# A tick of filler matmuls between the two pmx passes of quarter 2, and quarters 5, 8, 17 and 27 set to three ticks

## The chip, the cores and the metric

The kernel runs on one core of a Trainium2 chip. The metric is the device time of one execution in microseconds; shown is the median of several runs. Five engines work side by side, each through its own list of instructions in order: TensorE (PE), VectorE (DVE), ScalarE (ACT), GpSimd (POOL) and SyncE (SP), which issues most of the DMAs. An engine waits only where an instruction names a semaphore of another engine or of a DMA.

## The reference: what is computed

One layer over 1024 latent tokens (a grid of 16 rows by 64 columns) and 256 context tokens, model width 1024, all in float32. A modulated RMS norm is followed by one input projection, whose columns go to two branches: attention with 8 heads of 64 in a clamped 8x16 window, with a learned bias per offset and all context keys in the same softmax, and a gated short convolution. Each branch is multiplied by SiLU of its own gate; one output projection and a gated residual end the layer.

```python
h = rmsnorm(x, norm_g) * (1 + scale[:, None]) + shift[:, None]
q, k, v, za, u, bg, cg, zc = jnp.split(h @ w_in, SPLIT_POINTS, axis=-1)
attn = neighbourhood_attention(q, k, heads(v), kc, vc, rpb) * jax.nn.silu(za)
conv = bg * centred_short_conv(cg * u, conv_w, conv_b) * jax.nn.silu(zc)
x_new = x + gate[:, None] * (jnp.concatenate([attn, conv], axis=-1) @ w_out)
```

## The kernel before, in words

Every float32 product is made of three passes over operands split in a high and a low part (`mm3`, line 72). The program has four stages: modulation and norm of x (to about 78 us), the projections for q, k and v (to about 270 us), attention (to about 530 us), and the output projection.

**The attention stage** is a loop over n = 0 to 35 that calls `quarter(n)` (line 1074). A head has four quarters, so n = 4h + g works on quarter g of head h; and three steps of a software pipeline stand in one call. Quarter n computes new scores (PE tiles `pss` and `pc`, lines 1100 and 1105), adds the bias and keeps a running maximum (DVE, `sb` and `mx`, lines 1133 to 1141); for e = n - 2 it turns the maxima with the PE into tile `pmx` (first pass, line 1086), reduces them on DVE to `rm` (line 1088), spreads `rm` back over the partitions with the PE (second pass, line 1096), copies the result on ACT to `mg`, and takes exponentials (DVE subtractions `sc` and `sb`, ACT, low parts on POOL `plc` and DVE `pll`); for o = n - 3 it multiplies with the values (PE tile `po`). In this stage PE, ACT, DVE and POOL run in exactly the order in which the code records the instructions (`ordered`, line 44); SP's order is made by the framework's scheduler.

**The filler.** The PE work of attention is too short for the other engines' chain, so the rest of the projections (the gates z and the convolution's u, c, gate and b columns) is cut into ticks and put between. A unit (line 341) is one block of 128 columns: 8 ticks, each of two steps k with three matmuls of 512 columns, so six matmuls. Ticks 1 to 4 of a unit fill one tile `pu` (its first half of the tokens, k from 0 to 7), ticks 5 to 8 the next one. `pu` has two buffers (line 358), so tick 1 of a unit writes over the first half of the unit before. The units run in the order z0 to z3, and then for each of three convolution groups CU, CCG, ZC, CBG. `next(fill)` gives out one tick. Quarter n has `TICKS[n]` of them (line 33): from n = 1 on, one stands after the score matmuls (line 1116), the others after the `po` matmuls at the end of the quarter (line 1144). In total 110 ticks are given out.

**The chores.** A tick leaves work for other engines, put in two lists (`soon` and `slow`, line 302): ACT splits the next unit's weights (`uh<-uraw`), DVE takes the low part (`ul`), ACT copies products away (`z`, `ub`), DVE multiplies (`cu`, `cv`), ACT and DVE make the convolution's taps (`cv<-cu`), ACT applies SiLU (`zs<-pu`), for which it loads another function table and then loads the table of the exponential again. ACT does all of its chores at the end of a quarter (`do_acts`, line 1148), behind its exponentials. DVE does them early in the next quarter (`do_dves(3)`, line 1091): all of `soon` and up to three of `slow`, between `rm` and the subtraction `sc<-sc,mg`; a step of `gated` (line 1280) may add `ri`, or `zs` and `tb`, at the same place. So a tick that moves into another quarter takes its chores along.

With the table of before, 48 ticks have been given out at the end of quarter 16 and 80 at the end of quarter 26: there the first and the second ZC unit end, and the CBG units begin with quarters 17 and 27.

Of the kernel before, what the change touches and what calls it, by code (L numbers as in the profile page):

```python
# [29 lines left out]
CTXT = 3  # L30
FORDER = [4, 5, 6, 0, 1, 2, 3, 7]

TICKS = [2, 3, 3, 3, 3, 2, 3, 3, 2] + 2 * (8 * [3] + 2 * [4]) + 3 * [3] + [4, 4, 3, 2]
EPS = 1e-6


# [3 lines left out]
def body(tc, es, x, ctxt, w_ada, b_ada, w_in, q_g, k_g, rpbr, w_out, vecs, cst, out):  # L40
# [269 lines left out]
    def do_acts():  # L310
        for c in soon + (slow if not any(c[1] and c[1].__name__ == "product" for c in soon) else []):
            if c[0]:
                c[0]()
                c[0] = None

    def do_dves(most=99):
        for queue in chores:
            while queue and not queue[0][0] and (queue is soon or most > 0 and not soon):
                on_dve = queue.pop(0)[1]
                if on_dve:  # L320
                    on_dve()
                    most -= 1
# [730 lines left out]
    def pair_of(n):  # L1053

        h, g = divmod(n, 4)
        two = [(h, 0), (h - 1, 7)] if g == 0 else [(h, 2 * g - 1), (h, 2 * g)]
        return [(i, heads[h_], j) for i, (h_, j) in enumerate(two) if 0 <= h_ < NH]

    def both(v, n, pair):

        w = 256 if n % 4 == 0 else 384
        return v[:, pair[0][0]:pair[-1][0] + 1, :w]

    def maxima_of(n, pair):

        step, w = (768, 256) if n % 4 == 0 else (P, 384)
        lo = (2 * (n % 4) - 2) * P if n % 4 else pair[0][0] * step
        v = mg[:, lo:lo + w].rearrange("p (o c) -> p o c", o=1)
        if len(pair) == 1:
            return v  # L1070
        part = list(v.ap)
        return bass.AP(v.tensor, v.offset, [part[0], [step, 2], [1, w]])

    def quarter(n):

        live = lambda m: 0 <= m < 4 * NH
        ticks = TICKS[n]  # L1080
        e, o = n - 2, n - 3
        if live(e):
            hd, g = heads[e // 4], e % 4
            pm = psm.tile([P, 512], F32, name="pmx", tag="C", bufs=2)
            for i in range(2):
                pe.transpose(pm[:, i * P:(i + 1) * P], mx[:, (2 * g + i) * P:(2 * g + i + 1) * P], ident)
            rm = ap.tile([P, 2], F32, name="rm", tag="rm", bufs=8)
            dve.tensor_reduce(rm, pm[:, :256].rearrange("p (i k) -> p i k", i=2), AX.X, ALU.max)
        if live(o):
            heads[o // 4].ctx_out(o % 4)  # L1090
        do_dves(3)
        if gating and next(gating[0], "end"):
            gating.pop(0)
        if live(e):
            for i in range(2):
                pe.transpose(pm[:, 256 + i * P:256 + (i + 1) * P], rm[:, i:i + 1].broadcast_to([P, P]), ident)
            act.copy(mg[:, g * 256:(g + 1) * 256], pm[:, 256:512])
        now = pair_of(n)
        for i, hd_, j in now:
            hd_.scores(j, sbank[:, i])  # L1100
        if n == 0:
            next(fill)
            ticks -= 1
        if live(n):
            heads[n // 4].ctx_scores(n % 4)
        if live(e):
            hd.ctx_exp(g)
        if e in sbs or e in exps:
            pair, sb = pair_of(e), sbs.pop(e)
            w = both(sb, e, pair)  # L1110
            dve.tensor_tensor(w, w, maxima_of(e, pair), ALU.subtract)
            exps[e] = [ap.tile([P, 2, 384], F32R, name=m, tag=m, bufs=2) for m in ("phl", "pll")]
            ph, pl = (both(v, e, pair) for v in exps[e])
            act.activation(ph, w, AF.Exp)
            act.activation(w, w, AF.Exp)
        for _ in range(n > 0):
            next(fill, None)
        done = []
        if o >= 0:
            pho, plo = exps.pop(o)  # L1120
            for i, hd_, j in pair_of(o):
                hd_.lat_out(j, pho[:, i], plo[:, i])
                if j in (4, 7):
                    done.append((hd_, j // 7))
                    if j == 7 and hd_.s:
                        ready.append(hd_.p)
        if now:
            sb = sbs[n] = sb_new()
            g_ = n % 4
            if g_:  # L1130
                bt = now[0][1].bt
                bias = bt[:, 1:2].broadcast_to([P, 2, 384]) if g_ == 2 else bt[:, 0:2] if g_ == 1 else bt[:, 1:3]
                dve.tensor_tensor(sb, sbank[:, :, :384], bias, ALU.add)
            else:
                for i, hd_, j in now:
                    cols = slice(P, 384) if j == 0 else slice(0, 256)
                    dve.tensor_tensor(sb[:, i, :256], sbank[:, i, :256], hd_.bt[:, 1, cols], ALU.add)
            if live(n):
                heads[n // 4].ctx_max(n % 4)
            for i, hd_, j in now:  # L1140
                hd_.lat_max(j, sb[:, i])
        if e in sbs or e in exps:
            dve.tensor_tensor(pl, w, ph.bitcast(F32), ALU.subtract)
        for _ in range(ticks - (n > 0)):
            next(fill, None)
        for hd_, bank_ in done:
            hd_.finish(bank_)
        do_acts()
# [5 lines left out]
    def fillers():  # L1154
        for unit_ in [attn_group(f) for f in range(NPAIR)] + [conv_group(i) for i in range(1, 4)]:
            for got in unit_:
                if got is None:
                    yield
# [5 lines left out]
    fill = fillers()  # L1164
# [143 lines left out]
    with sbuf("att") as ap, psum("psb") as psb:  # L1308
# [6 lines left out]
        for n in range(4 * NH + 4):  # L1315
            h, g = divmod(n, 4)
            if 0 < h < NH and g == 0:
                heads[h].load_v()
            if h + 1 < NH and g:
                nx = heads[h + 1]  # L1320
                for load in ((nx.masks, nx.load_q), (nx.load_k,), ())[g - 1]:
                    load()
            quarter(n)
            if ready:
                p = ready.pop()
                if p < NPAIR - 1:
                    gating.append(gated(p))
                else:
                    recip(p, ap)
# [139 lines left out]
```

## Time and profile before

| | |
|---|---|
| median of 3 runs | 637.93 us (636.94 to 639.37) |
| the profiled execution's own time | 636.79 us |
| its span, first to last instruction | 635.0 us |
| mean granted TensorE clock | 0.999 |
| attention stage | about 270 to 530 us |

A row of the timeline gives the start in microseconds from the beginning of the span, the duration, the engine, the source line, the operation, the tiles it writes and reads with their shapes, how many equal ones were put together, and in brackets how long the engine stood idle before it and which engine's instruction ended that. Nearly all lines read L55, since the recording helper there issues every instruction: the tiles tell what it is. Matmuls overlap in the pipe, so the distance from start to start is the cost of one, not the shown duration. A quarter is recognised by its `pmx` rows: first pass `pmx<-ci,mx`, second pass `pmx<-ci,rm`; the first `pmx` rows of the stage belong to quarter 2.

### The profile page before, as it was taken

The numbers are of one execution on the slowest core, as the hardware profiler recorded it, in microseconds if no ns is written. First come the engines' busy times: TensorE is split into PE (matmuls) and PEld (weight loads), VectorE is DVE, ScalarE is ACT, GpSimd is POOL, SyncE is SP. The second block draws the span as 40 slices with busy tenths as digits, with TensorE's granted clock in tenths as the row PEclk, the third lists the DMA queues.
The fourth block names the chain that finished last, engine by engine and source line by source line (L and its number), as shares of the span: only waits on it lengthen the run. The fifth ranks groups of instructions, "written<-read, shape, count | busy, mean of one in ns | idle before, by whom it ended". The sixth has DMA issues, their size and how long they took to land.

```text
span 635.0 us, 10038 instructions
## 1 busy us (share of the span) xinstructions
PE 626.1 (99%) x3479; PEld 537.1 (85%) x3480; DVE 436.5 (69%) x819; ACT 324.1 (51%) x699; POOL 130.4 (21%) x140
## 2 busy tenths in 40 slices
PE   8999999999999999999999999999999999999997
PEld 3477899999899999888888888888888788888885
DVE  1677858765766845468898889988998964575111
ACT  3676835424624545345576658567775854451000
POOL 1305014123123222101122111111111112005221
PEclk9999999999999999999999999999999999999999
DMA  8972638866784994875383635683742233966421
GB/s 320 386 260 96 186 107 258 262 198 216 245 262 138 305 334 152 304 244 168 127 260 116 240 109 204 193 276 101 252 145 74 61 106 120 328 208 233 165 101 50
DMA packets 102863, 125.61 MB, mean 198 GB/s; under 512 B 9649, under 2 KB 71305, under 8 KB 101532
## 3 DMA queue, kind: packets, MB, share of 16 engines
q1 hardware_dynamic: 96348, 113.38, 53.9%
q10 hardware_dynamic: 6208, 11.05, 5.6%
q0 software_dynamic: 256, 0.54, 0.3%
q8 instruction: 27, 0.44, 0.3%
q14 instruction: 24, 0.20, 0.1%
HBM read 88.09 MB, written 38.62 MB: 200 GB/s over the span
## 4 chain that ended last, share of the span: by engine, by line
PE 91%; DVE 6%; ACT 1%; issue 1%; POOL 0%; DVEq 0%; ACTq 0%; POOLq 0%
PE pu L55 25%; PE pacc L55 21%; PE po L55 7%; PE acc L55 7%; PE tr L55 5%; PE pout L75 5%; PE pout L74 5%; PE pout L76 5%; PE cacc L55 4%; PE pss L55 3%; PE pmx L55 2%; DVE mx L55 2%; PE pc L55 2%; DVE sb L55 2%; PE trA L55 1%
## 5 line engine op out<-in xcount | busy, mean ns | idle before, releaser
L55 PE MATMUL pu<-h,uh 128*128 128x512 f32 x544 | 169.0, 392 | 0.0
L55 PE MATMUL pacc<-wh,h 128*128 128x384 f32 x512 | 135.1, 338 | 0.0
L55 PEld LDWEIGHTS pu<-h,uh 128*128 128x128 f32 x544 | 98.1, 188 | 16.9
L55 PE MATMUL pu<-h,ul 128*128 128x512 f32 x272 | 106.3, 391 | 0.0
L55 PEld LDWEIGHTS pacc<-wh,h 128*128 128x128 f32 x512 | 92.8, 188 | 0.1
L55 POOL TENSOR_TENSOR plc<-sc,phc 128x512 fp32r<-128x512 f32 x32 | 43.0, 1345 | 215.5 <-ACT sc L55 159.0
L55 PE MATMUL pacc<-wl,h 128*128 128x384 f32 x256 | 85.6, 334 | 0.0
L55 POOL TENSOR_TENSOR ss<-ss,few 128x4 f32<-128x4 f32 (+1 forms) x40 | 41.4, 1037 | 126.3 <-DVE ss L55 126.1
L55 DVE TENSOR_TENSOR mx<-mx,sb 128x384 f32<-128x384 f32 (+1 forms) x64 | 59.4, 936 | 2.0
L55 PEld LDWEIGHTS pu<-h,ul 128*128 128x128 f32 x272 | 51.1, 188 | 11.3
L75 PE MATMUL pout<-wol,yh 128*128 128x512 f32 x128 | 49.8, 389 | 0.0
L76 PE MATMUL pout<-woh,yl 128*128 128x512 f32 x128 | 49.5, 389 | 0.0
L74 PE MATMUL pout<-woh,yh 128*128 128x512 f32 x128 | 48.3, 389 | 0.0
L55 PEld LDWEIGHTS pacc<-wl,h 128*128 128x128 f32 x256 | 48.1, 188 | 0.1
L55 DVE TENSOR_REDUCE ss<-sq 128x4 f32<-128x260 f32 (+1 forms) x40 | 15.8, 394 | 42.4 <-ACT sq L55 42.4
L55 ACT ACTIVATE sq<-pacc 128x256 f32<-128x256 f32 x32 | 12.3, 384 | 54.4 <-PE pacc L55 53.9
L1401 DVE TENSOR_TENSOR ot<-pout,gate 128x512 f32<-128x512 f32 x16 | 10.8, 689 | 40.5 <-PE pout L76 37.7
L55 ACT COPY mg<-pmx 128x256 f32<-128x256 f32 x32 | 11.9, 372 | 51.9 <-PE pmx L55 45.3
L1402 POOL TENSOR_TENSOR ot<-ot,xr 128x512 f32<-128x512 f32 x15 | 20.0, 1345 | 68.2 <-DVE ot L1401 67.0
L55 ACT COPY sc<-pc 128x512 f32<-128x512 f32 x32 | 18.8, 588 | 25.5 <-PE pc L55 25.5
L55 ACT ACTIVATE qn<-pacc,ss 128x64 f32<-128x64 f32 x128 | 30.0, 329 | 3.0 <-issue 2.5
L55 DVE TENSOR_TENSOR pll<-sb,phl 128x768 fp32r<-128x768 f32 (+2 forms) x33 | 28.4, 861 | 4.5 <-ACT sb L55 4.5
(155 smaller groups left out, 1280.9 us busy)
## 6 DMA issues: line engine op xcount, KB each, us to landing
uraw<-in_w_in SPq DMA_DIRECT2D x34, 256.0 KB
q_d<-qs SPq DMA_DIRECT2D x32, 256.0 KB
k_s<-k_d SPq DMA_DIRECT2D x8, 1024.0 KB
q_s<-q_d SPq DMA_DIRECT2D x16, 512.0 KB
wr<-in_w_in SPq DMA_DIRECT2D x40, 192.0 KB
slab<-in_w_ada SPq DMA_DIRECT2D x6, 1024.0 KB
v_d<-vs SPq DMA_DIRECT2D x20, 260.0 KB
v<-v_d SPq DMA_DIRECT2D x16, 325.0 KB
```

The costliest lines, as they stand in the source:

```text
L55: i = emit(*a, **kw)
L74: i = pe.matmul(ps, ah, bh, start=first, stop=False)
L75: pe.matmul(ps, ah, bl, start=False, stop=False)
L76: pe.matmul(ps, al, bh, start=False, stop=last)
L1401: dve.tensor_tensor(ot, ps, gate[:, cols], ALU.mult)
L1402: (dve if (nh, t) == (1, NB - 1) else pool).tensor_tensor(ot, ot, xr, ALU.add)
```

## The change

The table of ticks is rewritten, and one branch is added in `quarter`:

```diff
-TICKS = [2, 3, 3, 3, 3, 2, 3, 3, 2] + 2 * (8 * [3] + 2 * [4]) + 3 * [3] + [4, 4, 3, 2]
+TICKS = [2] + 17 * [3] + [4] + 9 * [3] + [4] + 3 * [3] + [4, 4, 3, 2]
...
         if live(o):
             heads[o // 4].ctx_out(o % 4)
+        elif live(e):
+            next(fill)
+            ticks -= 1
         do_dves(3)
```

Written out, four entries differ: quarters 5 and 8 go from 2 to 3 ticks, quarters 17 and 27 from 4 to 3. The sum stays 110. So the filler is one tick ahead of before at the end of quarters 5 to 7, two at the end of 8 to 16, one at the end of 17 to 26, and level from the end of quarter 27 on. The new branch holds only for n = 2, where e = 0 exists and o = -1 does not: its first tick then stands between the two `pmx` passes, and its last one is left out.

PE in quarter 2 (`h_219` to `h_745` are the eight k of the normalised x, two to a tick):

```order
 L55 MATMUL pmx<-ci,mx 128x128 x2
+L55 MATMUL pu<-h_221,uh 128x512 x2
+L55 MATMUL pu<-h_221,ul 128x512
+L55 MATMUL pu<-h_222,uh 128x512 x2
+L55 MATMUL pu<-h_222,ul 128x512
 L55 MATMUL pmx<-ci,rm 128x128 x2
 L55 MATMUL pss<-q_s,k_s 128x384 x4
 L55 MATMUL pc<-q_s,kc_s 128x256 x4
-L55 MATMUL pu<-h_221,uh 128x512 x2
-L55 MATMUL pu<-h_221,ul 128x512
-L55 MATMUL pu<-h_222,uh 128x512 x2
-L55 MATMUL pu<-h_222,ul 128x512
```

The tick that stood behind the scores now stands before the second pass; the later ticks of the quarter follow one place earlier.

PE before, where the first CBG unit begins (`h_219` is k = 0): its first tick comes in quarter 17, behind the scores, and its first matmul waits for ACT.

```order
L55 MATMUL pss<-q_s,k_s 128x384 x4
L55 MATMUL pc<-q_s,kc_s 128x256 [waits PE_49]
L55 MATMUL pc<-q_s,kc_s 128x256 x3
L55 MATMUL pu<-h_219,uh 128x512 [waits Activation_49]
L55 MATMUL pu<-h_219,uh 128x512
L55 MATMUL pu<-h_219,ul 128x512
```

PE in the change: the same tick comes in quarter 16, behind that quarter's `po` matmuls (`h_745` is k = 7, the last step of the ZC unit).

```order
L55 MATMUL pu<-h_745,ul 128x512
L55 MATMUL po<-phl,v_3356 65x384 [waits Activation_49]
L55 MATMUL po<-phl,v_3356 65x384
L55 MATMUL po<-pll,v_3356 65x384
L55 MATMUL po<-phl,v_3356 65x384 x2
L55 MATMUL po<-pll,v_3356 65x384
L55 MATMUL pu<-h_219,uh 128x512 [waits Activation_49]
```

ACT in the change, quarter 16 from the copy of the context scores on, to the first row of quarter 17:

```order
L55 COPY sc<-pc 128x512 [waits PE_49,Pool_49]
L55 ACTIVATE phc<-sc 128x512 [waits DVE_49]
L55 ACTIVATE sc<-sc 128x512 [waits Activation_49]
L55 ACTIVATE phl<-sb 128x768 [waits DVE_49]
L55 ACTIVATE sb<-sb 128x768 [waits Activation_49]
L55 ACT_TABLE_LOAD
L55 ACTIVATE zs<-pu 128x512
L55 ACTIVATE zs<-pu 128x512 [waits PE_49]
L55 ACTIVATE zs<-zs 128x512 x2
L55 COPY mg<-pmx 128x256 [waits DVE_49,PE_49]
```

The SiLU of the ZC unit (`zs<-pu`) stays at the end of ACT's quarter 16, as before (there one `uh<-uraw` stood between `sb` and the table load), while PE's tick that writes over the buffer it reads has moved from quarter 17 into quarter 16. The second CBG unit goes the same way, from the first tick of quarter 27 to the last of quarter 26, and ACT's `uh<-uraw` ahead of that table load is gone too.

DVE before, quarter 25 from `rm` to the first subtraction and the maxima:

```order
L55 TENSOR_REDUCE rm<-pmx 128x2
L55 TENSOR_TENSOR cu<-pu,ub 128x4x16x8
L55 TENSOR_TENSOR zs<-zs,rb 128x512
L55 TENSOR_TENSOR tb<-tb,zs 128x512
L55 TENSOR_TENSOR sc<-sc,mg 128x512
```

DVE in the change, the same place:

```order
L55 TENSOR_REDUCE rm<-pmx 128x2
L55 TENSOR_SCALAR cv<-cu,vecT,cv 128x512 x3
L55 TENSOR_TENSOR zs<-zs,rb 128x512
L55 TENSOR_TENSOR tb<-tb,zs 128x512
L55 TENSOR_TENSOR sc<-sc,mg 128x512
```

The product `cu` has moved into quarter 24, and three taps of the convolution have come in for it. In the other quarters between 7 and 29 chores shift in the same manner by a quarter: in quarters 8, 11 and 21 one `ul` stands where two stood, quarters 13, 15 and 24 have one or two pieces more, quarter 27 has two products `cv<-zs` in place of one `ul` and two taps, and quarters 18, 19, 28 and 29 have one piece fewer. DVE's list in quarters 2 to 6 is unchanged.

## The prediction

> **What bounds the kernel now.** I read the page first, then the busy time of the attention stage, then the timeline of PE, DVE and ACT, quarter by quarter.
>
> ```profile
> PE 626.1 (99%) x3479; PEld 537.1 (85%) x3480; DVE 436.5 (69%) x819; ACT 324.1 (51%) x699; POOL 130.4 (21%) x140
> ...
> PE 91%; DVE 6%; ACT 1%; issue 1%; POOL 0%; DVEq 0%; ACTq 0%; POOLq 0%
> ```
>
> The PE is busy throughout and carries 91% of the chain that ended last; DVE has 6%. PE's amount of work does not change here. So the time moves only by stretches in which the PE stands still, and those lie where it waits for DVE in the attention stage:
>
> ```profile
> 256.00:530.00 274.00, 272.11 (x1548) 231.14 (x1547) 228.68 (x352) 171.18 (x293) 44.27 (x39) 1.00 0.53 172
> ```
>
> The columns are length, then PE, PE's weight loads, DVE, ACT, POOL. PE is busy for 272.1 of 274.0 us, but with matmuls that overlap; DVE for 228.7, or 83%: some 6.2 us of a usual quarter of 7.2 to 7.5. DVE is close to full, so it matters in which quarter its pieces stand.
>
> **Quarter 2.** The first pass, the second, a tick, and the next quarter's first pass on the PE; then DVE's first subtraction and the two maxima:
>
> ```profile
> 278.52 0.38 PE L55 MATMUL pmx<-ci,mx 128*128 128x128 f32 x2
> 279.42 0.43 PE L55 MATMUL pmx<-ci,rm 128*128 128x128 f32 x2 [0.52 <-DVE rm L55]
> ...
> 280.88 0.63 PE L55 MATMUL pu<-h,uh 128*128 128x512 f32 x2
> ...
> 282.27 0.62 PE L55 MATMUL pu<-h,uh 128*128 128x512 f32 x2
> ...
> 285.00 0.38 PE L55 MATMUL pmx<-ci,mx 128*128 128x128 f32 x2
> ```
> ```profile
> 280.29 0.69 DVE L55 TENSOR_TENSOR sc<-sc,mg 128x512 f32<-128x512 f32 x1 [0.33 <-ACT mg L55]
> ...
> 282.56 2.13 DVE L55 TENSOR_TENSOR mx<-mx,sb 128x384 f32<-128x384 f32 x2
> ```
>
> A tick costs 282.27 - 280.88, nearly 1.4 us (1.37 over several). Between the passes the PE stands 0.68 us (279.42 instead of 278.74, two matmuls of 0.11 after the first pass began). The tick put there fills this and overshoots: the second pass starts at 278.74 + 1.37 = 280.11, **0.69 later**. All that follows from it, `mg`, `sc`, the maxima, is a chain without slack and shifts by 0.69: the maxima end at 285.38 in place of 284.69. The next quarter's second `pmx` matmul (285.1 now) needs them, 0.06 later: 285.44. So the PE, which gets there earlier, waits for DVE, and quarter 3 runs 0.35 later than before. **+0.35**, where the wait taken away promised -0.68. Bounds: -0.68 if the chain had that slack, +0.69 if nothing absorbs.
>
> **Quarters 5 and 8.** They have two ticks, and the quarter after each starts late. Second passes of quarters 5 and 6, 8 and 9, and of the undisturbed 12 to 14:
>
> ```profile
> 300.35 0.41 PE L55 MATMUL pmx<-ci,rm 128*128 128x128 f32 x2
> ...
> 307.49 0.43 PE L55 MATMUL pmx<-ci,rm 128*128 128x128 f32 x2 [0.17 <-DVE rm L55]
> ```
> ```profile
> 322.26 0.42 PE L55 MATMUL pmx<-ci,rm 128*128 128x128 f32 x2
> ...
> 328.81 0.43 PE L55 MATMUL pmx<-ci,rm 128*128 128x128 f32 x2
> ```
> ```profile
> 351.04 0.41 PE L55 MATMUL pmx<-ci,rm 128*128 128x128 f32 x2
> ...
> 358.35 0.40 PE L55 MATMUL pmx<-ci,rm 128*128 128x128 f32 x2
> ...
> 365.88 0.41 PE L55 MATMUL pmx<-ci,rm 128*128 128x128 f32 x2
> ```
>
> Quarters repeat in kind every four. Quarter 5 to 6 takes 7.14 with two ticks, 13 to 14 (the same kind) 7.53 with three; so the third tick costs 0.39 and brings 1.37: **-0.98**. Quarter 8 to 9 takes 6.55, 12 to 13 takes 7.31: **-0.61**. DVE's pieces in 5 are the same, in 8 one fewer, so no new wait comes. From here on the PE is two ticks, 2.74 us of work, ahead.
>
> **Quarter 16: the PE waits for ACT.** Being two ahead, the first tick of CBG falls into quarter 16. It writes over the `pu` half that the ZC unit's SiLU reads, and that SiLU is ACT's last chore of the quarter. Now, on PE (second pass of 16, the first tick behind `po`, and the first tick of 17), DVE and ACT:
>
> ```profile
> 380.60 0.41 PE L55 MATMUL pmx<-ci,rm 128*128 128x128 f32 x2
> ...
> 384.23 0.62 PE L55 MATMUL pu<-h,uh 128*128 128x512 f32 x2
> ...
> 389.31 0.63 PE L55 MATMUL pu<-h,uh 128*128 128x512 f32 x2
> ```
> ```profile
> 382.48 0.68 DVE L55 TENSOR_TENSOR sc<-sc,mg 128x512 f32<-128x512 f32 x1
> ```
> ```profile
> 385.27 0.85 ACT L55 ACTIVATE sb<-sb 128x768 f32<-128x768 f32 x1
> 386.02 0.60 ACT L55 CAST uh<-uraw 128x512 fp32r<-128x512 f32 x1
> 386.64 1.28 ACT L55 ACT_TABLE_LOAD   x1
> 387.93 1.09 ACT L55 ACTIVATE zs<-pu 128x512 f32<-128x512 f32 x2
> ```
>
> Before, the tick in question came at 389.31, in quarter 17; the first SiLU (half of the 1.09 and a little) ended at 388.5, so the PE did not wait. In the change PE is there 384.23 - 380.60 = 3.63 after the second pass of 16. ACT's chain hangs on `sc`, 1.88 after that pass; `sb` ends 3.64 later; the `uh` between is gone; the table load takes 1.28 and a SiLU 0.57; with the hand-over 7.45 in all. The wait is 7.45 - 3.63: **+3.8**. Two ticks stand behind it, then the first pass of quarter 17, hence DVE's `rm`, ACT's `mg` and everything in that quarter: nothing else can fill it, for PE's list is fixed. Bounds: 0, if the SiLU were done by then, to 4.4, with the `uh` left in.
>
> The Trainium skill, page "ScalarE: Activation LUTs", section "What ACT_TABLE_LOAD costs", puts 1283 ns on the load and some 1380 ns of drain on every switch of tables. The load's row agrees; for the drain the rows leave no room (`uh` ends at 386.62, the load starts at 386.64, SiLU at 387.93). By the page both SiLU waits would be 1.4 us longer, by the trace not.
>
> **Quarter 25: DVE has too much.** Here quarter 27 of before shows the prices, for its list is nearly that of 25 in the change:
>
> ```profile
> 464.84 0.42 DVE L55 TENSOR_REDUCE rm<-pmx 128x2 f32<-128x256 f32 x1
> 465.18 0.68 DVE L55 TENSOR_TENSOR ul<-uraw,uh 128x512 fp32r<-128x512 f32 x1
> 465.78 1.53 DVE L55 SCALAR_TENSOR_TENSOR cv<-cu,vecT,cv 128x512 f32<-128x512 f32 x2
> 467.24 0.68 DVE L55 TENSOR_TENSOR zs<-zs,rb 128x512 f32<-128x512 f32 x1
> 467.95 0.69 DVE L55 TENSOR_TENSOR tb<-tb,zs 128x512 f32<-128x512 f32 x1
> 468.56 0.69 DVE L55 TENSOR_TENSOR sc<-sc,mg 128x512 f32<-128x512 f32 x1
> ...
> 473.81 0.42 DVE L55 TENSOR_REDUCE rm<-pmx 128x2 f32<-128x256 f32 x1
> ```
> ```profile
> 472.96 0.44 PE L55 MATMUL pmx<-ci,mx 128*128 128x128 f32 x2
> ...
> 474.28 0.43 PE L55 MATMUL pmx<-ci,rm 128*128 128x128 f32 x2 [0.17 <-DVE rm L55]
> ```
>
> From `rm` to `sc` 3.72; with a third tap (0.73, half of 465.78 to 467.24, and a little) for the `ul` (0.60) it is 3.9. From `sc` to the next `rm` 5.25, to the second pass 0.47 more: 9.6 from `rm` to second pass. Undisturbed it is 0.5 + 7.53 = 8.0. **+1.6** (0, if the PE's lateness gave DVE room, to 2).
>
> **Quarter 26: the second SiLU.** Second pass, the tick that is last in the quarter, `sc`, and ACT's end of `sb`:
>
> ```profile
> 457.81 0.41 PE L55 MATMUL pmx<-ci,rm 128*128 128x128 f32 x2
> ...
> 463.06 0.62 PE L55 MATMUL pu<-h,uh 128*128 128x512 f32 x2
> ```
> ```profile
> 459.70 0.68 DVE L55 TENSOR_TENSOR sc<-sc,mg 128x512 f32<-128x512 f32 x1
> ```
> ```profile
> 462.27 0.63 ACT L55 ACTIVATE sb<-sb 128x512 f32<-128x512 f32 x1
> ```
>
> PE arrives 5.25 after the second pass; `sb` ends at 5.09, load and SiLU take 1.85, hand-over 0.06: 7.0. **+1.7** (0 to 2.4).
>
> **Quarter 27** has three ticks now and lighter chores: two products of 0.60 for `ul` and two taps, 0.86 less on DVE, but the PE comes 1.37 earlier. Its second pass stands 0.40 late today (474.28 against 472.96 + 0.92); it will stand 0.9 late: **+0.5**. **The rest**: quarters 13, 15 and 24 get one or two pieces of 0.6 to 0.7 more on DVE and overrun by 0.2 to 0.5 each, the table load of the exponential delays quarter 17 a little, and a small wait at quarter 20 goes: **+1.0** as an estimate from these rows (0 to 2).
>
> **Sum**: 0.35 - 0.98 - 0.61 + 3.8 + 1.6 + 1.7 + 0.5 + 1.0 = +7.4. The profiled execution took 636.79 (its span 635.0 and 1.8 around it), so it would take 644.2; the median of the runs shown, 637.93, is 1.14 above it, so the forecast is **645.3**.
>
> **The rivals.** *The stalls of short quarters are all that counts* (the other side): the filled waits return 0.98 + 0.61, and 0.68 in quarter 2, and the shifted DVE pieces and the SiLU fit in idle time, DVE being 69% and ACT 51% busy: 635.7, faster. It decides if ACT reaches the SiLU before the PE's moved tick; the rows say 3.8 us after. Chance 0.06. *No wait for SiLU, but DVE overruns*: 645.3 - 5.5 = 639.8; 0.08. *PE's waits give DVE room*, so that the overruns vanish and only 0.35 - 1.59 + 5.5 remain: 642.2; 0.14. It speaks for it that a late PE lets DVE finish; against, that 25 lies far behind the wait in 16. *The clock falls in the wait*: 647.3; 0.10. At its start, after idle time, the same matmul runs at half its later rate:
>
> ```profile
> 1.38 2.74 PE L55 MATMUL acc<-warm 128*128 128x512 bf16 x6 [1.38 <-POOL warm L55]
> ...
> 15.47 1.24 PE L55 MATMUL acc<-warm 128*128 128x512 bf16 x5
> ```
>
> About 4 us at half rate would cost 2 us; the longest idle time later in this trace is under 1 us and shows no such thing, so a wait of 3.8 us is untried. The Trainium skill, "TensorE: Matmul & The Clock Gate", section "Part 1: The HAM clock gate", says that the clock halves after an idle window of some 3.4 us that runs freely; by that a wait of 3.8 us would seldom hold a whole window, and the time would mostly be the forecast's.
>
> **Chances.** The forecast has 0.62. A measurement here tells about 0.5% (3.2 us) from no change. Slower by more than that: 0.62 + 0.14 + 0.10, less a little of the second: 0.85. Within: 0.13. Faster: 0.02, for even the first rival gives only 0.35%. The range 641.5 to 648 takes in the forecast with its bounds, the case of 642.2 and the slower clock, and leaves out the two rivals without the SiLU wait.
>
> **What would show it.** Quarter 2: no wait before the second pass, one of about 0.3 before the next first pass for `mx`. Quarters 6 and 9: no wait of PE. Quarter 16: one idle time of 3 to 4 us before `pu`, ended by ACT's `zs`; quarter 26 one of about 1.7; second passes of 26 and 28 late by `rm`. It is wrong if PE shows no wait for `zs`, or if the waits are there and the rest of the stage shrinks by as much.

## The result, and the profile after

The changed kernel takes **648.09 us** (median of five runs, 647.76 to 648.29), the kernel before 637.93 us (636.94 to 639.37): a ratio of 1.0163, with an interval of 1.0152 to 1.0174. It is slower by 1.6%, 2.8 us more than the 645.3 forecast and 0.1 us above the range. The profiled execution took 647.99 us against 636.79, its span is 646.2 us against 635.0, and the mean granted TensorE clock is 0.994 against 0.999.

From the page of the changed kernel, the busy times, the chain that ended last, and the costliest group, whose last column is the idle time ahead of it:

```profile
PE 630.3 (98%) x3479; PEld 539.3 (83%) x3480; DVE 435.8 (67%) x819; ACT 324.2 (50%) x699; POOL 131.0 (20%) x140
...
PE 85%; DVE 7%; ACT 4%; issue 2%; DMA 1%; POOL 0%; SPq 0%; ACTq 0%; DVEq 0%; POOLq 0%
...
L55 PE MATMUL pu<-h,uh 128*128 128x512 f32 x544 | 171.2, 396 | 5.1 <-ACT zs L55 5.1
```

ACT's share of the chain rose from 1% to 4%, and the products wait 5.1 us for `zs`. The same number of matmuls is busy 4.2 us longer (630.3 against 626.1); part of this is matmuls that became slower, as the rows show, and a wait alone doesn't do that.

PE around quarter 16, from the timeline: its second pass, the last `po`, the first tick of CBG, and the first two passes of quarter 17:

```profile
383.29 0.43 PE L55 MATMUL pmx<-ci,rm 128*128 128x128 f32 x2 [0.18 <-DVE rm L55]
...
386.77 0.34 PE L55 MATMUL po<-pll,v 128*65 128x384 f32 x1
390.78 1.22 PE L55 MATMUL pu<-h,uh 128*128 128x512 f32 x2 [3.67 <-ACT zs L55]
...
392.22 1.05 PE L55 MATMUL pu<-h,uh 128*128 128x512 f32 x2
...
393.50 1.05 PE L55 MATMUL pu<-h,uh 128*128 128x512 f32 x2
...
396.06 0.46 PE L55 MATMUL pmx<-ci,mx 128*128 128x128 f32 x2
...
397.05 0.42 PE L55 MATMUL pmx<-ci,rm 128*128 128x128 f32 x2
```

The PE stands 3.67 us, released by ACT's `zs`. Then three matmuls take 1.28 us (392.22 to 393.50), 0.43 each, where a matmul of a tick at full clock takes 1.37 / 6 = 0.23. The twelve up to the first pass of quarter 17 take 5.28 us instead of 2.74. ACT in the same time:

```profile
387.97 0.84 ACT L55 ACTIVATE sb<-sb 128x768 f32<-128x768 f32 x1
388.83 1.28 ACT L55 ACT_TABLE_LOAD   x1
390.13 1.09 ACT L55 ACTIVATE zs<-pu 128x512 f32<-128x512 f32 x2
```

`sb`, table load and SiLU stand end to end as forecast, without a gap at the switch of tables; the first SiLU ends half-way through the 1.09 us and the PE starts. The granted clock, in stretches of 1 us (columns as in the prediction's row of this view: length, PE, weight loads, DVE, ACT, POOL, then the clock, third from the end):

```profile
388.00:389.00 1.00, 0.00 (x0) 0.00 (x0) 1.00 (x2) 0.98 (x2) 0.61 (x1) 1.00 1.00 301
389.00:390.00 1.00, 0.00 (x0) 0.00 (x0) 1.00 (x2) 1.00 (x1) 0.00 (x0) 0.69 1.09 327
390.00:391.00 1.00, 0.22 (x1) 0.23 (x2) 0.09 (x1) 0.99 (x3) 0.00 (x0) 0.50 0.96 351
...
396.00:397.00 1.00, 1.00 (x9) 0.90 (x7) 0.45 (x2) 0.00 (x0) 0.00 (x0) 0.90 0.00 0
```

The clock fell to half at about 389.4, inside the wait, and rose again at 396.2, after 6.8 us; the PE worked through 5.4 of them.

Quarter 2, and the second passes of quarters 6 and 9:

```profile
279.32 0.38 PE L55 MATMUL pmx<-ci,mx 128*128 128x128 f32 x2
...
280.93 0.38 PE L55 MATMUL pmx<-ci,rm 128*128 128x128 f32 x2
...
286.20 0.33 PE L55 MATMUL pmx<-ci,mx 128*128 128x128 f32 x1 [0.83 <-DVE mx L55]
...
309.04 0.41 PE L55 MATMUL pmx<-ci,rm 128*128 128x128 f32 x2
...
331.09 0.41 PE L55 MATMUL pmx<-ci,rm 128*128 128x128 f32 x2
```

The wait before quarter 2's second pass is gone and one of 0.83 us for the maxima stands in the next quarter; in 6 and 9 no wait is left. Quarters 25 to 28 on the PE:

```profile
458.58 0.43 PE L55 MATMUL pmx<-ci,rm 128*128 128x128 f32 x2
...
465.89 0.30 PE L55 MATMUL pmx<-ci,mx 128*128 128x128 f32 x1 [0.53 <-DVE mx L55]
...
467.59 0.43 PE L55 MATMUL pmx<-ci,rm 128*128 128x128 f32 x2 [0.16 <-DVE rm L55]
474.49 0.73 PE L55 MATMUL pu<-h,uh 128*128 128x512 f32 x2 [1.47 <-ACT zs L55]
...
483.78 0.30 PE L55 MATMUL pmx<-ci,mx 128*128 128x128 f32 x1 [0.44 <-DVE mx L55]
...
485.49 0.43 PE L55 MATMUL pmx<-ci,rm 128*128 128x128 f32 x2 [0.17 <-DVE rm L55]
```

Quarter 25 takes 9.01 us from second pass to second pass, quarter 26 has the second wait for `zs`, and quarter 28 waits for DVE. Behind the wait of 1.47 us a pair of matmuls took 0.73 us, against 1.22 behind the wait of 3.67: here the clock stayed full.

**Where the time went**, from second pass to second pass. Each entry is the distance from the second pass of the quarter before to that of the quarter named (for quarter 2, from its first pass), less the same distance before, less 1.372 us for each tick by which the quarter before has more than in the kernel before (or 1.372 added for each fewer). Quarters not named moved by 0.07 or less.

| second pass of quarter | forecast | after | branch only | table only | 5 and 17 | 8 and 27 | 16 filled | 4 filled | 10 filled | halves | tap out |
|---|---|---|---|---|---|---|---|---|---|---|---|
| 2 and 3 | +0.35 | 0.34 | 0.34 | 0.00 | 0.00 | -0.01 | 0.34 | 0.35 | 0.36 | 0.35 | 0.34 |
| 6 | -0.98 | -0.98 | 0.01 | -0.98 | -0.98 | 0.00 | -0.99 | -0.96 | -0.98 | -0.98 | -0.96 |
| 9 | -0.61 | -0.62 | -0.01 | -0.62 | 0.00 | -0.63 | -0.62 | -0.62 | -0.62 | -0.62 | -0.62 |
| 16 | rest | 0.41 | 0.00 | 0.41 | 0.47 | 0.47 | 0.41 | 0.42 | 0.41 | 1.06 | 0.41 |
| 17 | +3.8 | **6.47** | 0.01 | 5.49 | 3.95 | 2.44 | 3.99 | 5.58 | 3.98 | 0.03 | 5.59 |
| 18, 20, 25 | rest | 0.53 | 0.00 | 0.56 | 0.16 | 0.16 | 0.48 | 0.50 | 0.51 | 0.49 | 0.50 |
| 26 | +1.6 | 1.46 | 0.00 | 1.46 | 0.00 | 1.46 | 1.46 | 1.46 | 1.46 | 1.46 | 0.67 |
| 27 | +1.7 | 1.78 | -0.03 | 1.77 | 0.00 | 1.80 | 1.77 | 1.77 | 1.77 | 0.80 | 1.77 |
| 28 | +0.5 | 1.01 | -0.01 | 1.00 | -0.01 | 1.01 | 1.01 | 1.01 | 1.02 | 1.03 | 1.02 |

All steps of the changed kernel add up to 10.4 us; another 0.8 had come up before quarter 2 (279.32 against 278.52), where nothing was changed: it is the profiled executions' own difference.

### The profile page after: what moved, and what is told of

Same layout as the page of the kernel before. It is cut to its first block, busy times and chain, and to the rows that moved or that the text cites. A ratio compares the mean times of both kernels' runs of the same rounds, so it can differ in the third digit from the quotient of the medians.

```text
span 646.2 us, 10041 instructions
## 1 busy us (share of the span) xinstructions
PE 630.3 (98%) x3479; PEld 539.3 (83%) x3480; DVE 435.8 (67%) x819; ACT 324.2 (50%) x699; POOL 131.0 (20%) x140
## 4 chain that ended last, share of the span: by engine, by line
PE 85%; DVE 7%; ACT 4%; issue 2%; DMA 1%; POOL 0%; SPq 0%; ACTq 0%; DVEq 0%; POOLq 0%
PE pu L55 23%; PE pacc L55 21%; PE acc L55 6%; PE po L55 6%; PE tr L55 5%; PE pout L76 4%; PE pout L74 4%; PE pout L75 4%; PE cacc L55 4%; PE pss L55 2%; DVE mx L55 2%; PE pmx L55 2%; PE pc L55 2%; DVE sb L55 2%; PE trA L55 1%
## 5 line engine op out<-in xcount | busy, mean ns | idle before, releaser
L55 PE MATMUL pu<-h,uh 128*128 128x512 f32 x544 | 171.2, 396 | 5.1 <-ACT zs L55 5.1
## 6 DMA issues: line engine op xcount, KB each, us to landing
uraw<-in_w_in SPq DMA_DIRECT2D x34, 256.0 KB
q_d<-qs SPq DMA_DIRECT2D x32, 256.0 KB
```

The lines of the kernel that those rows point to most:

```text
L55: i = emit(*a, **kw)
```

## The experiments

The theory after the result, called A below: the loss is the two SiLU waits, a halved clock behind the first, and the overfull lists of DVE in quarters 25 and 27. Each ratio is to the kernel before in the same batch (medians of 637.4 to 637.8).

### The branch alone, and the table alone

```diff
         if live(o):
             heads[o // 4].ctx_out(o % 4)
+        elif live(e):
+            next(fill)
+            ticks -= 1
```

> The kernel before with the new branch alone (one tick of quarter 2 between its two pmx passes), the old table of ticks. Theory A (the chain from the second pass through mg, sc and the maxima has no slack, so the overshoot of the tick is partly passed on): quarter 3 runs about 0.35 us later, 638.3 us, a ratio of 1.0005. Rival (the 0.68 us in which PE stood between the passes are simply filled): 637.25 us, ratio 0.999. Both are small beside a measurement; the rows decide: by A quarter 2's second pass stands 0.7 later after its first pass than in before and a wait for mx of some 0.8 us appears ahead of quarter 3's pmx.

Measured: 637.89 us, ratio 1.0007 (0.9998 to 1.0016). The time cannot tell 0.35 us from none; the row does. PE in the kernel with the branch alone, quarter 3's first pass:

```profile
286.20 0.33 PE L55 MATMUL pmx<-ci,mx 128*128 128x128 f32 x1 [0.82 <-DVE mx L55]
```

It waits for the maxima, and the step is +0.34 as in the change. The rival's gain of 0.68 isn't there.

```diff
-TICKS = [2, 3, 3, 3, 3, 2, 3, 3, 2] + 2 * (8 * [3] + 2 * [4]) + 3 * [3] + [4, 4, 3, 2]
+TICKS = [2] + 17 * [3] + [4] + 9 * [3] + [4] + 3 * [3] + [4, 4, 3, 2]
```

> The new table of ticks alone, quarter 2 as in before. Theory A (nearly all of the loss is the table's: the SiLU waits, the slowed clock and the DVE overruns): 648.09 - 0.35 = 647.7 us. Rival (the branch's gain of 0.68 stands inside the change): 648.8 us. A further rival, that branch and table add up to the loss only together (PE's lateness of quarter 2 carried on): clearly less, under 646 us. By A the granted clock falls to about 0.5 behind the idle time of quarter 16 here too.

Measured: 646.64 us (645.82 to 647.69), ratio 1.0147 (1.0134 to 1.0160), a microsecond under the expectation. Every step is that of the change except the one into quarter 17, 5.49 against 6.47, behind the same wait of 3.68 us: the clock was low for less of the work. The loss is the table's; how much of it the clock takes varies from run to run (mean clock 0.994 to 0.997 here, 0.994 in each run of the changed kernel).

### One early tick instead of two

Quarter 5 with three ticks and 17 with three; then quarter 8 with three and 27 with three:

```diff
-TICKS = [2, 3, 3, 3, 3, 2, 3, 3, 2] + 2 * (8 * [3] + 2 * [4]) + 3 * [3] + [4, 4, 3, 2]
+TICKS = [2, 3, 3, 3, 3, 3, 3, 3, 2, 3, 3, 3, 3, 3, 3, 3, 3, 3, 4, 3, 3, 3, 3, 3, 3, 3, 3, 4, 4, 3, 3, 3, 4, 4, 3, 2]
```
```diff
-TICKS = [2, 3, 3, 3, 3, 2, 3, 3, 2] + 2 * (8 * [3] + 2 * [4]) + 3 * [3] + [4, 4, 3, 2]
+TICKS = [2, 3, 3, 3, 3, 2, 3, 3, 3, 3, 3, 3, 3, 3, 3, 3, 3, 4, 4, 3, 3, 3, 3, 3, 3, 3, 3, 3, 4, 3, 3, 3, 4, 4, 3, 2]
```

> The kernel before with quarter 5 at three ticks and quarter 17 at three, nothing else: the filler is one tick ahead from quarter 5 to quarter 16, so the first CBG tick is the last tick of quarter 16 and is one tick of 1.37 us further from the second pass than in the change; the table of quarters 17 to 35 is as before from then on. Theory A: quarter 5 to 6 gives -0.98; the wait for SiLU in quarter 16 is 3.8 - 1.37 = 2.4 us, which is too short an idle time for the clock to fall; with 0.4 of shifted DVE pieces the time is 637.9 - 1.0 + 2.4 + 0.4 = 639.7 us, mean granted clock as in before. Rival (any wait of some 2 us at this place halves the clock behind it): some 2 us more, 641.7 us, and slow matmuls behind the wait. Rival (the slow matmuls of the change come from DMA or engine contention of its order and not from the idle time): slow matmuls here without a long wait.

> The kernel before with quarter 8 at three ticks and quarter 27 at three, nothing else: the filler is one tick ahead from quarter 8 to 26. Theory A: quarter 8 to 9 gives -0.6; the SiLU waits are 2.4 us in quarter 16 and 1.7 in quarter 26; the lists of DVE in quarters 18 to 28 are those of the change, so quarter 25 to 26 costs 1.5, 27 to 28 costs 1.0, and other shifted pieces 0.7: 637.9 + 6.7 = 644.6 us (643.6 to 645.2), clock full. Rival (the DVE overruns of quarters 25 and 27 come only with the lateness that quarter 16 brings): 642.1 us. Rival (clock falls also in a wait of 2.4 us): 646.6 us.

Measured: 641.14 us (639.41 to 643.00), ratio 1.0058 (1.0043 to 1.0073), and 645.66 us (643.65 to 647.44), ratio 1.0140 (1.0126 to 1.0155). Both lie above A's figures, and their runs spread as those of before do not. The two profiles show why. PE's first CBG tick and the clock behind it, in the kernel with quarters 5 and 17 changed:

```profile
389.68 1.22 PE L55 MATMUL pu<-h,uh 128*128 128x512 f32 x2 [2.12 <-ACT zs L55]
```
```profile
390.00:394.00 4.00, 4.00 (x17) 3.28 (x17) 0.93 (x2) 1.15 (x3) 0.00 (x0) 0.63 0.95 386
```

And with quarters 8 and 27 changed:

```profile
389.23 0.73 PE L55 MATMUL pu<-h,uh 128*128 128x512 f32 x2 [2.13 <-ACT zs L55]
```
```profile
390.00:394.00 4.00, 4.00 (x27) 3.55 (x26) 2.85 (x5) 1.73 (x5) 0.00 (x0) 1.00 0.84 348
```

The same wait halved the clock in one execution and left it alone in the other. The share of the DMA engines is 0.95 where the clock fell and 0.84 where it didn't, so these two rows alone don't rule out the DMA; the rows of the next experiment do. In the first kernel four runs of six had a mean clock of 0.996 or 0.997 and took 641.1 to 643.0, two had 1.000 and took 639.4 and 639.5, close to A's 639.7. In the second, two of four had 0.996 and took 646.2 and 647.4, the others 643.7 and 645.2. So A held for the wait and failed for the clock: 2.1 us can be enough. In the second kernel quarters 25 and 27 cost 1.46 and 1.01 though quarter 16 cost only 2.44. That speaks against the rival that ties them to that lateness; the kernel with the SiLU of each half, below, settles it: they cost 1.46 and 1.03 there, where quarter 16 cost 0.03.

### Filling the wait

```diff
+        if n == 16:
+            junk = psm.tile([P, 512], F32, name="junk", tag="C", bufs=2)
+            for _ in range(16):
+                pe.matmul(junk, hh[0][:, :P], hh[0][:, :512], start=True, stop=True)
         for _ in range(ticks - (n > 0)):
             next(fill, None)
```

and the same with 4 and with 10 in place of 16.

> The changed kernel with sixteen added matmuls of 512 columns in quarter 16, between its po matmuls and its two last ticks; nothing reads their result. They take about 3.6 us at full rate, so the PE works through most of the time in which it stood and waited for SiLU. Theory A (the PE's own idle time of 3.7 us lowered the clock): the clock stays full, the twelve matmuls behind the wait run at 0.23 us each, and the time falls by 2.5 us to 645.6 in spite of the added work. Rival (the slow matmuls have another cause, such as DMA traffic or the engines that run beside them): the twelve stay at 0.43 us, 648.1 us.

> The changed kernel with four added matmuls of 512 columns in quarter 16 at the same place; nothing reads their result. They take 0.9 us and leave an idle time of some 2.8 us ahead of the first CBG tick. Theory A (the clock falls only after more than some 3 us without work): full clock, 645.6 us. Rival (a wait of 2 us or more at this place is enough): the clock still falls, 648 us, or some part of it.

> The changed kernel with ten added matmuls of 512 columns in quarter 16 ahead of its two last ticks; nothing reads their result. They leave an idle time of about 1.4 us ahead of the first CBG tick. Theory A, as it stands after the runs with waits of 2.1 and 2.75 us (the clock falls when some 2 us of a stretch of 3.4 us are idle, wherever the stretch begins): no run falls, 645.4 us. Rival (any wait ahead of the CBG tick can bring the clock down, only less often the shorter it is): some runs 1.5 us longer with a mean clock of 0.997 or less.

Measured: with sixteen 645.22 us (645.07 to 646.71), ratio 1.0127 (1.0112 to 1.0141); with ten 645.43 us (645.36 to 645.90), 1.0121 (1.0108 to 1.0134); with four 646.56 us (645.26 to 648.46), 1.0136 (1.0120 to 1.0151). PE and its clock with sixteen:

```profile
386.53 3.81 PE L55 MATMUL junk<-h 128*128 128x512 f32 x16
390.37 0.73 PE L55 MATMUL pu<-h,uh 128*128 128x512 f32 x2
```
```profile
390.00:394.00 4.00, 3.96 (x21) 3.08 (x20) 0.35 (x2) 1.85 (x4) 0.00 (x0) 1.00 0.84 341
```

Added work made the kernel faster, by 2.3 us (from the ratios) to 2.9 (from the medians). Nothing else in quarter 16 changed, the clock stays full, and the step into quarter 17 is 3.99 instead of 6.47: the slow matmuls came from the PE's own idle time, and 2.5 us of the loss is the clock. With ten a wait of 1.40 us is left, and the clock stays full in all four runs (0.998 to 1.000):

```profile
390.67 0.73 PE L55 MATMUL pu<-h,uh 128*128 128x512 f32 x2 [1.40 <-ACT zs L55]
```

With four, a wait of 2.75 us, the clock fell, against A's figure. PE, and the clock in stretches of 1 us:

```profile
391.09 0.74 PE L55 MATMUL pu<-h,uh 128*128 128x512 f32 x2 [2.75 <-ACT zs L55]
```
```profile
391.00:392.00 1.00, 0.91 (x4) 0.77 (x5) 0.00 (x0) 1.00 (x4) 0.00 (x0) 1.00 1.00 407
392.00:393.00 1.00, 1.00 (x5) 0.82 (x4) 0.00 (x0) 0.57 (x2) 0.00 (x0) 0.71 0.98 406
...
395.00:396.00 1.00, 1.00 (x6) 0.80 (x5) 0.07 (x1) 0.00 (x0) 0.00 (x0) 0.58 0.00 0
```

Here it fell at about 392.4, 1.3 us after the PE had begun to work again, and rose at 395.8, 3.4 us later; in the changed kernel it stayed low for 6.8 us, twice that. So what lowers it looks at a stretch that is not tied to the wait's own start. Nor is it the DMA: at 391 its share (the last column but one) is 1.00 and the clock is full, at 395 it is 0.00 and the clock is still low.

The traces also show which stretch it is. In the changed kernel the clock falls at 389.38, rises at 396.21, and falls again at the end of the program, at 645.38: 6.83 and 256.0 us after the first fall, which is 2 and 75 times 3.413 us. In all five profiled executions whose clock fell in quarter 16 (the changed kernel, the table alone, quarters 5 and 17, four filled, and the tap left out, below) these distances are whole multiples of 3.413. Laid out on this grid, the stretch that ends with the fall holds 2.02 to 3.41 us without a matmul, and no stretch of the attention stage with 1.61 us or less ends with one. In the kernel with quarters 8 and 27 changed an edge of the grid, at 388.1, cuts the wait of 2.13 us into 1.01 and 1.12, and the clock stays full. In the changed kernel the stretch after the fall still holds 1.40 us of the wait, and the clock stays low to its end and through the next. So a wait of some 2 us lowers the clock if it lies in one stretch, and doesn't if an edge divides it.

### The SiLU of each half at once

```diff
             for got in unit(z_col(4 + i)):
                 if got:
-                    z.append(got)
+                    chore(lambda ps=got[1]: one(zs, ps))
...
-            chore(lambda: zs.extend(silus(z)))
...
+    def one(zs, ps):
+        zs.append(cvp.tile([P, 512], F32, name="zs", tag="ub", bufs=2))
+        act.activation(zs[-1], ps, AF.Silu)
+        if len(zs) == 2:
+            silus(())
```

> The changed kernel with the SiLU of each half of a ZC unit as a chore of its own, taken as soon as that half is finished, in place of both at the end of the unit: the first half's SiLU then stands some quarters earlier, at the price of one more pair of table loads per convolution group (three more pairs). Theory A (PE waits in quarters 16 and 26 because the SiLU of the first half stands last in the same quarter): both waits go and with them the slow clock, -3.8 - 2.5 - 1.8; the table loads cost up to 1.4 us in all where they delay mg: 641.3 us (640.5 to 642.5). Rival (the waits only change their releaser, for instance to the second half's pu or to DVE): 645 us or more.

Measured: 641.35 us (641.04 to 641.74), ratio 1.0060 (1.0048 to 1.0073), as A has it. The step into quarter 17 falls from 6.47 to 0.03 and no PE wait for `zs` is left; the step into quarter 16 pays 0.65 for the added table loads. The step into quarter 27 keeps 0.80, where PE waits for DVE's maxima ahead of its first pass. This too is a price of the added table loads: one of them, with its SiLU, now stands ahead of `uh` on ACT, and DVE waits for that in quarter 26:

```profile
462.44 0.69 DVE L55 TENSOR_TENSOR ul<-uraw,uh 128x512 fp32r<-128x512 f32 x1 [0.82 <-ACT uh L55]
```

Together the two are 1.45 us, at the bound of 1.4 that A allowed for the table loads.

### One tap left out of quarter 25

```diff
             def outer():
+                if now_n[0] == 25:
+                    now_n[0] = 0
+                    return
                 v = cvs[half][:].rearrange("p (r c) -> p r c", r=16)
```

(`now_n[0]` is set to n at the start of each quarter.)

> The changed kernel with one of the three taps that DVE takes in quarter 25 left out of the computation. Theory A (quarter 25 is late because DVE's list is longer than the quarter): the second pass of quarter 26 comes 0.73 us earlier, its step falls from 1.46 to 0.73 us, and nothing later takes it back: 647.4 us. Rival (the lateness comes from the order on PE or ACT and the list of DVE has room): quarter 26 as in the change, 648.1 us.

Measured: 645.79 us (644.41 to 647.03), ratio 1.0125 (1.0108 to 1.0141). DVE in quarter 25 of that kernel:

```profile
456.98 1.40 DVE L56 SCALAR_TENSOR_TENSOR cv<-cu,vecT,cv 128x512 f32<-128x512 f32 x2
...
459.63 0.68 DVE L56 TENSOR_TENSOR sc<-sc,mg 128x512 f32<-128x512 f32 x1
```

The step into quarter 26 falls from 1.46 to 0.67, by 0.79 for a tap of 0.73, and the others stay: quarter 25 is bound by the length of DVE's list. The total fell by more, below the 647.4 expected: in the profiled execution the step into quarter 17 is 5.59 instead of 6.47, which is the clock again (its mean was 0.995 to 0.999 in these runs), and 0.55 us lies ahead of quarter 2.

### Two tries for a faster version

First, another table without the branch, in which the units end a quarter earlier than before, so that SiLU and CBG's first tick stand apart as they did:

```diff
-TICKS = [2, 3, 3, 3, 3, 2, 3, 3, 2] + 2 * (8 * [3] + 2 * [4]) + 3 * [3] + [4, 4, 3, 2]
+TICKS = [2, 3, 3, 4, 3, 3, 3, 3, 3, 3, 3, 3, 3, 3, 3, 3, 3, 3, 4, 3, 3, 3, 3, 3, 3, 4, 3, 4, 3, 3, 3, 3, 4, 4, 2, 1]
```

> The kernel before with another table and without the branch: quarter 3 has four ticks, quarters 5 and 8 have three, and the second ticks that before had in quarters 17, 18 and 27 stand elsewhere, so that 48 ticks are given out at the end of quarter 15 and 80 at the end of quarter 25. Then each unit boundary coincides with the end of a quarter one quarter earlier than in before, and the first CBG tick stands behind the scores of the next quarter as in before, a whole table load and SiLU after ACT's chore. Theory A (the gains of quarters 5 and 8 are real, the loss comes from the place of the SiLU alone): 637.9 - 1.6 = 636.3 us, no wait for zs. Rival (the shifted DVE chores cost as much as in the change): 639 us or more.

(By the table, quarters 3 and 25 have four ticks, 5, 8, 17 and 28 have three, 34 and 35 one fewer than before; 18 and 27 keep four.)

Measured: 639.78 us (639.12 to 640.70), ratio 1.0035 (1.0023 to 1.0048): the rival's figure. The gains of quarters 6 and 9 are there (-0.96 and -0.62) and no wait for `zs` in the attention stage, but the second pass of quarter 16 comes 0.41 late, 17 1.40, 18 0.59, 24 0.89 and 27 1.13 (4, 25, 28 and 32 take back 0.24 to 0.47 each). The dearest of them, at 17, does not have the rival's cause. DVE in quarter 16 of that kernel, and the PE's second pass of quarter 17:

```profile
390.95 0.96 DVE L55 TENSOR_TENSOR pll<-sb,phl 128x768 fp32r<-128x768 f32 x1 [1.29 <-ACT sb L55]
```
```profile
392.30 0.43 PE L55 MATMUL pmx<-ci,rm 128*128 128x128 f32 x2 [0.75 <-DVE rm L55]
```

ACT is late with `sb`, DVE with `pll` and `rm`, and the PE waits. The table loads and the SiLU of a ZC unit delay the next quarter's exponentials; before, that quarter was 17, with four ticks, and no wait stood ahead of the second pass after it (396.78).

Second, the table of before with three ticks in 5, 8, 17 and 18, and the first half of a ZC unit copied out of `pu` as soon as it is done:

```diff
+                    if len(z) == 1 and not done:
+                        chore(lambda: early(z, zs))
...
+    def early(z, zs):
+        zs.append(cvp.tile([P, 512], F32, name="zs", tag="ub", bufs=2))
+        act.copy(zs[0], z[0][1])
...
-TICKS = [2, 3, 3, 3, 3, 2, 3, 3, 2] + 2 * (8 * [3] + 2 * [4]) + 3 * [3] + [4, 4, 3, 2]
+TICKS = [2] + 26 * [3] + [4, 4] + 3 * [3] + [4, 4, 3, 2]
```

> The kernel before with quarters 5 and 8 at three ticks and quarters 17 and 18 at three (one tick more than before from quarter 5, two from 8 to 16, one at 17, level from 18 on), without the branch; and the first half of a ZC unit is copied by ACT out of pu into zs as soon as it is finished, the SiLU at the end of the unit then works on that copy in place, so the first CBG tick has nothing to wait for. Theory A (the SiLU that holds the first half of pu is the only price of being ahead, beside the small DVE overrun of quarter 15; the overruns of 25 and 27 belong to the ticks that were shifted there): -0.98 - 0.62 + 0.41 + 0.35 - 0.18 = -1.0, 636.4 us, full clock. Rival (the copy and what it delays on ACT, or another wait at quarter 17, eats the gain): 637.4 us or more.

Measured: 637.30 us (636.58 to 639.97) against 637.77, ratio 0.9994 (0.9983 to 1.0004): no difference that these runs can tell. The copy does what it should, for quarter 17 comes 0.03 late; but quarters 16, 18 and 19 come 0.61, 0.72 and 0.33 late, and 20 takes back 0.15, so that 1.5 of the 1.6 gained is gone:

```profile
401.08 0.43 PE L55 MATMUL pmx<-ci,rm 128*128 128x128 f32 x2 [0.17 <-DVE rm L55]
```

With three ticks the quarter behind the SiLU waits for DVE. No version here beats the kernel before.

## Why the prediction was wrong

**Quarter 2** (+0.35) was right: +0.34, in the change and with the branch alone. Only the sign given for it was misread, a wait of about 0.3 ahead of the next first pass: the wait is 0.83, for PE gets there earlier than before; 0.34 is what is left of it in the step. **Quarters 5 and 8** were right to 0.02 in every kernel that has them.

**Quarter 16** is the step that failed: a SiLU wait at full clock, +3.8, where +6.5 came. The wait itself was right: PE stood 3.67 us, and with the idle time filled the step is 3.99. (A step is some 0.3 longer than the wait shown, in quarter 26 too, since the wait is counted from the end of the last matmul, while without it the next one starts before that end, and since the first pair behind a wait takes 0.73 us at full clock instead of 0.62.) What was left out of the sum is the clock. It was named as a rival, with 647.3 us, and given only 0.10, with a rule standing beside it: the Trainium skill, "TensorE: Matmul & The Clock Gate", section "Part 1: The HAM clock gate", says that the clock falls after an idle window of about 3.4 us that runs freely, and I read from it that a wait of 3.8 us would seldom hold a whole window. The runs differ from that reading: waits of 3.7 us lowered the clock in all five runs of the changed kernel, and waits of 2.1 us in six runs of ten, so less than a whole idle window suffices: 2.02 us of one did, in the kernel with quarters 5 and 17 changed. That the window runs freely, and its length, agree with the runs: low stretches of 3.4 and 6.8 us, a fall up to 1.3 us after the wait, and the grid of 3.413 us. The size given to the rival, 2 us, was near the 2.5 measured.

**Quarter 25** (+1.6) came to 1.46, and leaving a tap out shows that DVE's list is the cause. **Quarter 26** (+1.7) came to 1.78 with a PE wait of 1.47. **The rest** (+1.0, an estimate) came to 0.41 at quarter 16, 0.53 at 18, 20 and 25, and about nothing elsewhere.

**Quarter 27** (+0.5) came to 1.01. The forecast took the time from `sc` to the next `rm` as before, 5.25 us; it was 5.75. DVE, POOL and ACT in quarter 27 of the changed kernel:

```profile
479.27 0.68 DVE L55 TENSOR_TENSOR sc<-sc,mg 128x512 f32<-128x512 f32 x1
...
482.06 2.17 DVE L55 TENSOR_TENSOR mx<-mx,sb 128x384 f32<-128x384 f32 x2
...
485.02 0.42 DVE L55 TENSOR_REDUCE rm<-pmx 128x2 f32<-128x256 f32 x1
```
```profile
481.93 1.30 POOL L55 TENSOR_TENSOR plc<-sc,phc 128x512 fp32r<-128x512 f32 x1 [9.16 <-ACT sc L55]
```
```profile
479.20 1.28 ACT L55 ACT_TABLE_LOAD   x1
480.50 0.63 ACT L55 ACTIVATE phc<-sc 128x512 fp32r<-128x512 f32 x1
```

And in quarter 27 of the kernel before:

```profile
471.35 1.67 DVE L55 TENSOR_TENSOR mx<-mx,sb 128x384 f32<-128x384 f32 x2
```
```profile
470.71 1.30 POOL L55 TENSOR_TENSOR plc<-sc,phc 128x512 fp32r<-128x512 f32 x1 [7.57 <-ACT sc L55]
```
```profile
467.63 1.28 ACT L55 ACT_TABLE_LOAD   x1
...
469.28 0.63 ACT L55 ACTIVATE phc<-sc 128x512 fp32r<-128x512 f32 x1 [0.37 <-DVE sc L55]
```

The maxima are 0.50 longer, and they lie beside POOL's `plc` for 1.17 us instead of 0.66, 0.51 more. `plc` comes behind ACT's exponentials, and these start 1.23 us after DVE's `sc` (480.50 against 479.27) instead of 0.72 (469.28 against 468.56): DVE's shorter list brings `sc` earlier, but before it was `sc` that ACT waited for, and now it is the table load. The relation holds beyond this quarter: of the 48 maxima of 128x384 in the changed kernel's trace, the 22 that lie beside `plc` for 0.66 to 1.20 us take that time and 0.41 to 0.42 us more, and the other 26 (beside it for 0.41 us at most) take 0.56 each. This fits the Trainium skill, "SBUF — State Buffer", section "Terms", by which VectorE and GpSimd share a pair of ports that one holds for a whole instruction while the other stands; no run here moved `plc` alone, so that the ports are the reason is argued, not shown.

The sum: 7.4 was forecast for the profiled execution, and its steps add up to 10.4; 2.5 is the clock and 0.5 quarter 27. The median of the runs is 2.8 above the forecast.

The rivals without a SiLU wait were wrong, as the rows show. *PE's waits give DVE room* was wrong too: quarters 25 and 27 cost the same in every kernel that has their lists, whatever quarter 16 cost.

## What to carry to other kernels

When a piece of the bound engine's work is moved ahead, look for the buffer that it writes over and for the last reader of that buffer on the other engines: the gain here was 1.6 us, the wait for that reader 3.7. A wait of the PE of some 2 us or more may cost more than its own length: price the slower clock behind it too (1.5 to 2.5 us in these executions), and if the wait can't be removed, work without use put into it can be cheaper than idling. A long quarter that looks wasteful may be what hides another engine's rare piece, such as a switch of tables.

## What was not expected of the hardware

- The granted clock went to 0.5 after waits of 2.1 to 3.7 us: by the mean clock of the runs (under 0.998) in 13 of 14 at 3.7 us (the changed kernel, the table alone, the tap left out), in three of four at 2.75 us, in six of ten at 2.1 us, in none of four at 1.4 us. It stayed low for 3.4 us or twice that, and the fall came from 2.0 us after the wait's start (quarters 5 and 17 changed: 387.56 and 389.58) to 1.3 us after its end, at an edge of a grid of 3.413 us with at least 2.02 us of idle time in the stretch before it.
- Sixteen added matmuls made the changed kernel 2.3 to 2.9 us faster.
- Two maxima of DVE took 2.17 or 1.67 us with the same shapes; the difference is the time that POOL's `plc` lay beside them (1.17 and 0.66 us).
